# Two expert products whose matmuls keep their written order

## The chip, the cores and the metric

The kernel runs on one core of one Trainium2 chip. What is measured is the device time of one execution in microseconds (us). The kernel before was timed three times: 1403.73, 1405.36 and 1406.20 us, a median of 1405.36 us.

## The reference

One encoder block for 256 tokens of width 1024, all in float32: a conditioned RMS norm, a mixer (a gated delta rule with 8 heads beside a short convolution), a residual, a second norm, a mixture of experts, a residual and a last norm. Only the experts matter here. A router picks 4 of 32 experts for each token; each expert is two products with a clamped SwiGLU between them:

```
gu = x_blk @ w1[e] + b1[e]                  # 1024 -> 2048
gate, up = split(gu, 2)
gate = min(gate, 7); up = clip(up, -7, 7)
act = gate * sigmoid(1.702 * gate) * (up + 1)
y = act @ w2[e] + b2[e]                     # 1024 -> 1024
```

Every expert's 12 MiB of weights (8 MiB of w1, 4 MiB of w2) is read once, so the 32 experts need 384 MiB from HBM.

## The kernel before, in words

The program is written in a tile framework. It traces the whole kernel, and then a scheduler chooses the order of the instructions on each engine: it plays the program through a model of the engines and the transfers, and on each engine it takes next what its model says is ready, by priority. An instruction that went through `pin` (line 84, the scheduler's `keep_in_program_order`) keeps its written order with the other pinned instructions of its engine; unpinned ones may be put anywhere between them that their data allow. Semaphores are added by the framework.

The mixer runs up to about 430 us. After that come the experts, two at a time, in 16 pairs (p = 0 to 15; two pairs share a group q of gathered tokens). A pair's 128 token slots are four blocks of 32; `owners` says which of the pair's two experts owns each block (two and two, or three and one).

- First product (`w1_pair`, lines 1372 to 1388). For each of eight row blocks k of w1, two transfers of 1 MiB are issued, one for each expert (m = 0, 1). Then, for each of four column quarters c and each of four slot blocks j, a matmul multiplies 32 tokens (stationary operand, 128x32) with 512 columns of the owner's weights (moving operand, 128x512). Block j stands at column position 32*j of the array (`tile_position=(0, 32 * j)`), and its output in partitions 32*j to 32*j+31 of the bank `pss[c]`. A float32 matmul shows as two matmul records, so one k is 32 records and a whole first product 256.
- SwiGLU on VectorE and ScalarE, then `to_ff` (lines 1390 to 1398): eight transposes on TensorE and two copies to the tile `aT`.
- Second product (`w2_pair`, lines 1417 to 1435): four chunks c of two transfers of 1 MiB, and for each chunk two row blocks, two halves h of 512 columns and four blocks j: 128 records. Then the outputs are scaled, weighted by the gates in `combine` (line 1404, eight records) and added to x1.
- The last pair's second product is `w2_cols` (lines 1437 to 1458), in three parts of 512, 256 and 256 columns with transfers of 512 and 256 KiB. Its matmuls are pinned already.

The written order (lines 1600 to 1616) is first product of p, second product of p - 1, `to_ff` of p; at the end second product of 14, first product of 15, `to_ff` of 15, `w2_cols`. Between these stand, unpinned, the bias matmuls that open the banks (line 119), the gather of the next group's tokens (line 1315, into one buffer XT), and the transposes of the gates (line 1347). Weights go to 18 tiles of 1 MiB in turn (`w_half`, lines 954 to 963); their transfers are all issued from SyncE's queue (SP), and a transfer is issued when the matmuls that read its tile's last content are done. Part of pairs 0 and 1 is loaded while the mixer runs.

Already pinned on TensorE, besides `w2_cols`, are some matmuls of the mixer, the first bias and ranking matmuls and the single-block gathers of pair 0. All stand in the written order ahead of, or between, the matmuls that the change touches.

Of the kernel before, what the change touches and what calls it, by code (L numbers as in the profile page):

```python
# [21 lines left out]
KT = D // 128  # L22
# [31 lines left out]
def encoder_block(ctx, tc, x, c, ada_w, ada_b, norm1_w, w_in, conv_qkv_w, a_log, dt_bias, onorm_w,  # L54
# [3 lines left out]
    V, A, G, PE = nc.vector, nc.scalar, nc.gpsimd, nc.tensor  # L58
# [25 lines left out]
    pin = tc.keep_in_program_order  # L84
# [28 lines left out]
    def acc():  # L113
        return pm.tile([128, 512], FT, name="acc", tag=next(accs), bufs=3)

    def w1_bias(pa, bsel, b1c, pss, parts=(0, 1, 2, 3), first=False, pinned=False):
        for c in parts:
            b = 32 * c
            i = PE.matmul(pss[c], bsel[b:b + 32, pa * 128:(pa + 1) * 128], b1c[b:b + 32], start=first, stop=not first,
                          tile_position=(b, 0), skip_group_check=True)  # L120
            if pinned:
                tc.keep_in_program_order(i)
# [9 lines left out]
    with ExitStack() as mix:  # L132
# [218 lines left out]
        for j in range(4):  # L351
# [12 lines left out]
            w = ep.tile([128, KT, 256], FT, name="raw", tag="raw", bufs=6) \  # L364
# [13 lines left out]
            for kk in range(2):  # L378
                k = 2 * j + kk
# [574 lines left out]
        def w_half():  # L954
            i = half_n[0] % (NHALF + 7)
            half_n[0] += 1
            if i < NHALF - 2 or NHALF <= i < NHALF + 2:
                return wp_box[0].tile([128, 2, 2, 512], FT, name="wst", tag="wst").rearrange("p a b n -> p (a b n)")
            if i == NHALF - 2:
                pair_box.append(wp_box[0].tile([128, 2, 2, 2, 512], FT, name="wst", tag="pair", bufs=1))  # L960
            if i < NHALF:
                return pair_box[-1][:, i - NHALF + 2].rearrange("p a b n -> p (a b n)")
            return (h_tile if i - NHALF - 2 in (0, 1) else raw_tile)([128, 2048], FT, "wst")
# [10 lines left out]
        def w1_load(p, k, regs):  # L974
            w = pre.pop((p, k), []) if p < 2 else []
            for m in range(len(w), 2):
                w.append(quarters(w1_tile(p, k, m, regs)[0]))
            return w
# [302 lines left out]
    for k, m, ts in ((KT - 2, 0, [fw, spare("pg"), spare("pgT")]), (KT - 2, 1, [spare("aT", 1024), spare("aT", 1024)]),  # L1281
                     (KT - 1, 0, [spare("g"), spare("g"), spare("u"), spare("th")]),
                     (KT - 1, 1, [spare("ysb"), spare("ysb"), e4])):
        c, qs = 0, []
# [23 lines left out]
    def gather_part(P, xq, ks):  # L1308
        p = misc()
        for kk, k in enumerate(ks):  # L1310
            o = p[:, kk * QS:(kk + 1) * QS]
            n = 0
            for t in range(2):
                for hx in (h2h, h2l):
                    i = PE.matmul(o, hx[:, t, k * 128:(k + 1) * 128], P[:, t],
                                  start=n == 0, stop=n == 3, skip_group_check=True)
                    n += 1
                    if len(ks) == 1:
                        pin(i)
            if k % 2:  # L1320
                V.tensor_scalar(xq[:, k], o, afc[:, k:k + 1], mod[:, 24 + k:25 + k], op0=OP.mult, op1=OP.add)
            else:
                A.activation(xq[:, k], o, AF.Identity, scale=afc[:, k:k + 1], bias=mod[:, 24 + k:25 + k])  # L1323

    def xq_tile():
        return work.tile([128, KT, QS], FT, name="XT", tag="XT", bufs=1)
# [25 lines left out]
    def owners(q):  # L1352
        return [m for m, g in enumerate(GROUPS[min(q, 1)]) for _ in range(g)]

    def swiglu(n, g_ps, u_ps):
        g = work.tile([128, 512], FT, name="g", tag="g", bufs=2)
        u = work.tile([128, 512], FT, name="u", tag="u", bufs=1)
        th = work.tile([128, 512], FT, name="th", tag="th", bufs=1)
        V.tensor_scalar(g[:n], g_ps[:n], 7.0, None, op0=OP.min)  # L1359
        A.activation(th[:n], g[:n], AF.Tanh, scale=0.851)  # L1360
        V.tensor_scalar(u[:n], u_ps[:n], 7.0, -7.0, op0=OP.min, op1=OP.max)
        V.scalar_tensor_tensor(g[:n], u[:n], 1.0, g[:n], op0=OP.add, op1=OP.mult)
        V.scalar_tensor_tensor(g[:n], th[:n], 1.0, g[:n], op0=OP.add, op1=OP.mult)
        return g
# [7 lines left out]
    def w1_pair(p, xq, bsel, pss, regs, mid):  # L1372
        q, pa = divmod(p, 2)
        own = owners(q)[4 * pa:4 * pa + 4]
        if p:
            w1_bias(pa, bsel, b1c, pss, first=True)
        for k in range(KT):
            w = w1_load(p, k, regs)
            for c in range(4):
                for j in range(4):  # L1380
                    PE.matmul(pss[c][j * 32:(j + 1) * 32], xq[:, k, (4 * pa + j) * 32:(4 * pa + j + 1) * 32],  # L1381
                              w[own[j] % 2][c], start=False, stop=k == KT - 1,
                              tile_position=(0, 32 * j), skip_group_check=True)
            if p == 0 and k < KT - 2:
                gather_part(P0, xq, (k + 2,))
            if k == 3:
                mid()
        return [swiglu(128, pss[half], pss[2 + half]) for half in range(2)]
# [11 lines left out]
    def combine(gt, ysb, c0, n):  # L1400
        for t in range(2):
            p = misc()
            for pa in range(len(ysb)):
                PE.matmul(p[:, 0:n], gt[pa][:, t], ysb[pa], start=pa == 0, stop=pa == len(ysb) - 1)  # L1404
            xv = x1[:, t, c0:c0 + n]
            V.tensor_tensor(xv, xv, p[:, 0:n], op=OP.add)  # L1406

    def w2_rows(p, m, regs):
        return moe_w2[0, 2 * p + m:2 * p + m + 1] if p < 2 else moe_w2[0, ds(regs[2 * (p % 2) + m], 1)]

    def scaled(ps, c0, n):
        y = work.tile([128, 512], FT, name="ysb", tag="ysb", bufs=2)[:, 0:n]
        V.tensor_tensor(y, ps[:, 0:n], gtf_box[0][:, c0:c0 + n], op=OP.mult)  # L1413
        return y


    def w2_pair(p, aT, gt, regs):
        q, pa = divmod(p, 2)
        own = owners(q)[4 * pa:4 * pa + 4]
        ys = [acc() for _ in range(2)]  # L1420
        for c in range(4):
            w = []
            for m in range(2):
                t = w_half()
                nc.sync.dma_start(t, w2_rows(p, m, regs)[:, 256 * c:256 * c + 256].rearrange("e (p i) n -> p (e i n)", i=2))
                w.append(t.rearrange("p (i n) -> p i n", i=2))
            for i in range(2):
                f = 2 * c + i
                for h in range(2):
                    for j in range(4):  # L1430
                        PE.matmul(ys[h][j * 32:(j + 1) * 32], aT[:, f, j * 32:(j + 1) * 32],  # L1431
                                  w[own[j] % 2][:, i, 512 * h:512 * h + 512], start=f == 0, stop=f == KT - 1,
                                  tile_position=(0, 32 * j), skip_group_check=True)
        for h in range(2):
            combine([gt[:, pa]], [scaled(ys[h], 512 * h, 512)], 512 * h, 512)

# [97 lines left out]
    xq = xq_tile()  # L1534
# [37 lines left out]
    def first_product(p):  # L1572
        nonlocal xq, bsel
        q, pa = divmod(p, 2)
        nxt = []
        if pa == 0 and q:
            _, regs[q] = nc.values_load_multi_w_load_instructions(
                pidx_i[0:1, 4 * q:4 * q + 4], engines=[mybir.EngineType.SP], min_val=0, max_val=NE - 1)

        def mid():  # L1580
            if p == 2:
                final_row()
            if pa == 1:
                if q + 1 < NQ:
                    gts[q] = gates_of(q)
                if q + 1 < NQ:
                    nxt.append(slots_of(q + 1))

        gs[p] = w1_pair(p, xq, bsel, [acc() for _ in range(4)] if p else pss0, regs[q], mid)
        if p == 0:  # L1590
            route_rest()
        if nxt:
            xq = gather(nxt.pop())
            bsel = bias_rows(q + 1)

    def second_product(p):
        w2_pair(p, aTs.pop(p), gts[p // 2], regs[p // 2])
# [22 lines left out]
    with tc.If(n_over > 0):  # L1620
        ov = work.tile([128, KT, 128], FT, name="over", tag="aT", bufs=2).rearrange("p b n -> p (b n)")
        V.tensor_tensor(rks[:, 0], rks[:, 0], capr[:, None, :].to_broadcast([128, 2, NE]), op=OP.subtract)
        with tc.For_i(0, NE, 1) as cp:
# [6 lines left out]
            with tc.For_i(0, nb, 1) as b:  # L1630
# [23 lines left out]
                for half in range(2):  # L1654
                    pss = [acc() for _ in range(2)]
                    for gu in range(2):
                        bs = slice(32 * (2 * gu + half), 32 * (2 * gu + half) + 32)
                        PE.matmul(pss[gu][0:32], ohe[bs].to_broadcast([NE, 32]), b1c[bs],
                                  start=True, stop=False, tile_position=(bs.start, 0), skip_group_check=True)
                    for k in range(KT):  # L1660
# [5 lines left out]
                        for gu in range(2):  # L1666
                            PE.matmul(pss[gu][0:32], xo[:, k], wo[:, gu], start=False, stop=k == KT - 1,
                                      skip_group_check=True)
                    act_t(32, swiglu(32, *pss), aTo[:, half * 4:half * 4 + 4, :])
                for half in range(2):  # L1670
                    y = acc()
                    for f in range(KT):
# [5 lines left out]
                                  skip_group_check=True)  # L1678
# [48 lines left out]
```

## Time and profile before

| | |
|---|---|
| median of three runs | 1405.36 us |
| the profiled execution | 1404.75 us |
| its span, first to last instruction | 1402.8 us |
| mean granted TensorE clock | 0.985 |
| TensorE matmul (PE) busy | 1358.1 us, 97% |
| TensorE weight load (PEld) busy | 692.8 us, 49% |
| VectorE / ScalarE / GpSimd busy | 513.4 / 279.4 / 151.0 us |
| HBM read | 486.82 MB |

The span is what the trace covers; the execution was 1.95 us longer. Busy time of an engine is the union of its instructions, so matmuls that run side by side in the array count once: a busy TensorE isn't necessarily a full one. A weight load or matmul whose number of columns is 32 uses a quarter of the array's columns. Granted clock 1.00 is the level of 2.4 GHz, 0.50 that of 1.2 GHz. DMA share is the mean busy share of the core's 16 DMA engines.

### The profile page before, as it was taken

How to read it: one execution, taken by the hardware profiler on the slowest of the kernel's cores; microseconds unless marked ns; L12 is line 12 of the kernel's file. 1: busy time of each engine (PE TensorE's matmuls, PEld its weight loads, DVE VectorE, ACT ScalarE, POOL GpSimd, SP SyncE). 2: the span in 40 equal slices, each digit the busy share in tenths (PEclk: the TensorE clock that was granted, in tenths of full speed). 3: DMA queues.
4: the chain of work that ended last, by engine and by line, in shares of the span. 5: the costliest groups of instructions: out<-in, count | busy, mean ns of one | idle time of the engine just before them, and what ended most of it. 6: DMA issues, size and time to landing. Idle time of an engine off the chain costs nothing. (4 is left out here: it accounts for less than half of the span.)

```text
span 1402.8 us, 24525 instructions
## 1 busy us (share of the span) xinstructions
PE 1358.1 (97%) x10250; PEld 692.8 (49%) x10251; DVE 513.4 (37%) x1018; ACT 279.4 (20%) x545; POOL 151.0 (11%) x126
## 2 busy tenths in 40 slices
PE   6999998999999999999999999999999999999996
PEld 4988897999994333233233333333333333333322
DVE  3387879876763322221203112120311212031112
ACT  3555553543642110010000000000000000000001
POOL 4555684000100000000000000000000000000000
PEclk9999999999998999999999999999999999999997
DMA  9968876346797899999999999999999999999990
GB/s 336 302 226 290 282 242 218 98 147 237 282 376 282 360 408 394 403 421 420 421 421 420 421 421 421 420 421 421 420 415 420 421 400 421 421 416 413 421 337 32
DMA packets 134708, 492.68 MB, mean 351 GB/s; under 512 B 11070, under 2 KB 68799, under 8 KB 86977
## 3 DMA queue, kind: packets, MB, share of 16 engines
q1 hardware_dynamic: 130548, 486.08, 88.0%
q10 hardware_dynamic: 4045, 4.98, 1.1%
q8 instruction: 82, 1.34, 0.4%
q14 instruction: 33, 0.27, 0.1%
HBM read 486.82 MB, written 4.21 MB: 350 GB/s over the span
## 5 line engine op out<-in xcount | busy, mean ns | idle before, releaser
L1381 PE MATMUL acc<-wst,XT 128*32 128x512 f32 x4088 | 543.4, 597 | 0.0
L1381 PEld LDWEIGHTS acc<-wst,XT 128*32 128x32 f32 x4088 | 153.8, 110 | 350.4 <-issue 341.0
L1431 PE MATMUL acc<-wst,aT 128*32 128x512 f32 x1920 | 244.7, 599 | 0.0
L313 PE MATMUL mm<-hh,wl 128*128 128x256 f32 (+1 forms) x520 | 149.3, 288 | 4.9 <-DVE wl L263 3.6
L311 PE MATMUL mm<-hh,wh 128*128 128x256 f32 (+1 forms) x520 | 151.3, 291 | 1.2 <-DVE cacc L556 1.2
L312 PE MATMUL mm<-hl,wh 128*128 128x256 f32 (+1 forms) x520 | 149.4, 287 | 0.0
L1359 DVE TENSOR_SCALAR g<-acc 128x512 f32<-128x512 f32 x32 | 21.5, 687 | 326.2 <-PE acc L1381 323.0
L1431 PEld LDWEIGHTS acc<-wst,aT 128*32 128x32 f32 x1920 | 68.4, 110 | 142.2 <-issue 136.0
L262 ACT CAST wh<-raw 128x1024 fp32r<-128x1024 f32 (+1 forms) x89 | 91.8, 1038 | 93.8 <-PE mm L312 55.0
L88 POOL TENSOR_TENSOR rs<-ss,half_m 128x2 f32<-128x2 f32 x3 | 2.1, 702 | 975.3 <-DVE ss L1689 910.7
L311 PEld LDWEIGHTS mm<-hh,wh 128*128 128x128 f32 (+1 forms) x520 | 100.2, 193 | 12.5 <-issue 8.1
L313 PEld LDWEIGHTS mm<-hh,wl 128*128 128x128 f32 (+1 forms) x520 | 99.9, 192 | 7.1 <-DVE wl L263 3.8
L312 PEld LDWEIGHTS mm<-hl,wh 128*128 128x128 f32 (+1 forms) x520 | 100.2, 193 | 0.9 <-issue 0.8
L1397 ACT ACTIVATE aT<-misc 128x512 f32<-128x512 f32 x32 | 17.9, 595 | 409.6 <-PE misc L1396 409.5
L263 POOL TENSOR_TENSOR wl<-raw,wh 128x1024 fp32r<-128x1024 f32 x36 | 87.7, 2444 | 71.7 <-ACT wh L262 65.7
L1413 DVE TENSOR_TENSOR ysb<-acc,gtf 128x512 f32<-128x512 f32 (+1 forms) x33 | 22.3, 675 | 147.5 <-PE acc L1431 132.7
L1406 DVE TENSOR_TENSOR x<-x,misc 128x512 f32<-128x512 f32 (+1 forms) x66 | 44.3, 671 | 84.6 <-PE misc L1404 84.6
L263 DVE TENSOR_TENSOR wl<-raw,wh 128x1024 fp32r<-128x1024 f32 (+1 forms) x53 | 63.8, 1208 | 24.2 <-ACT wh L262 23.9
L1360 ACT ACTIVATE th<-g 128x512 f32<-128x512 f32 x32 | 20.1, 629 | 250.2 <-DVE g L1359 209.9
L1404 PE MATMUL misc<-ysb,pgT 128*128 128x512 f32 (+1 forms) x132 | 64.7, 608 | 2.0 <-DVE ysb L1413 1.9
L1323 ACT ACTIVATE XT<-misc,mod,afc 128x256 f32<-128x256 f32 x32 | 16.9, 563 | 172.4 <-PE acc L1381 120.8
L556 DVE SCALAR_TENSOR_TENSOR cacc<-mm,col,cacc 128x254 f32<-128x254 f32 (+1 forms) x96 | 46.0, 480 | 9.0 <-ACT cacc L553 6.9
(391 smaller groups left out, 1424.5 us busy)
## 6 DMA issues: line engine op xcount, KB each, us to landing
wst<-in_moe_w_dram SPq DMA_DIRECT2D x372, 1024.0 KB, 16.6
raw<-in_w_in_dram SPq DMA_DIRECT2D x36, 1024.0 KB, 7.6
raw<-in_ada_w_dram SPq DMA_DIRECT2D x24, 1024.0 KB, 8.5
wst<-in_moe_w_dram SPq DMA_DIRECT2D x24, 256.0 KB, 6.7
wst<-in_moe_w_dram SPq DMA_DIRECT2D x11, 512.0 KB, 15.4
raw<-in_w_out_sc_dram SPq DMA_DIRECT2D x4, 1024.0 KB
raw<-in_w_up_a_dram SPq DMA_DIRECT2D x4, 1024.0 KB, 5.3
raw<-in_w_o_dram SPq DMA_DIRECT2D x4, 1024.0 KB, 10.2
```

Of the source, the lines that this page charges most:

```text
L262: a = A.copy(wh, src)
L263: b = (V if job.lo == "v" else G).tensor_tensor(wl, src, wh.bitcast(FT), op=OP.subtract)
L311: PE.matmul(ps, wh[:, k, :], ah[:, k, :], start=k == 0, stop=False, skip_group_check=True)
L312: PE.matmul(ps, wh[:, k, :], al[:, k, :], start=False, stop=False, skip_group_check=True)
L313: PE.matmul(ps, wl[:, k, :], ah[:, k, :], start=False, stop=k == KT - 1, skip_group_check=True)
L556: V.scalar_tensor_tensor(a[:, o0:o1], p[:, s0:s1], cw(j), a[:, o0:o1], op0=OP.mult, op1=OP.add)
L1359: V.tensor_scalar(g[:n], g_ps[:n], 7.0, None, op0=OP.min)
L1381: PE.matmul(pss[c][j * 32:(j + 1) * 32], xq[:, k, (4 * pa + j) * 32:(4 * pa + j + 1) * 32], w[own[j] % 2][c], start=False, stop=k == KT - ...
L1404: PE.matmul(p[:, 0:n], gt[pa][:, t], ysb[pa], start=pa == 0, stop=pa == len(ysb) - 1)
L1406: V.tensor_tensor(xv, xv, p[:, 0:n], op=OP.add)
L1413: V.tensor_tensor(y, ps[:, 0:n], gtf_box[0][:, c0:c0 + n], op=OP.mult)
L1431: PE.matmul(ys[h][j * 32:(j + 1) * 32], aT[:, f, j * 32:(j + 1) * 32], w[own[j] % 2][:, i, 512 * h:512 * h + 512], start=f == 0, stop=f == ...
```

## The change

Both inner matmuls go through `pin`, so the scheduler has to keep them in the written order, among themselves and with the other pinned instructions of TensorE. No instruction, operand, tile or transfer is added or removed.

```
             for c in range(4):
                 for j in range(4):
-                    PE.matmul(pss[c][j * 32:(j + 1) * 32], xq[:, k, (4 * pa + j) * 32:(4 * pa + j + 1) * 32],
-                              w[own[j] % 2][c], start=False, stop=k == KT - 1,
-                              tile_position=(0, 32 * j), skip_group_check=True)
+                    pin(PE.matmul(pss[c][j * 32:(j + 1) * 32], xq[:, k, (4 * pa + j) * 32:(4 * pa + j + 1) * 32],
+                                  w[own[j] % 2][c], start=False, stop=k == KT - 1,
+                                  tile_position=(0, 32 * j), skip_group_check=True))
...
                 for h in range(2):
                     for j in range(4):
-                        PE.matmul(ys[h][j * 32:(j + 1) * 32], aT[:, f, j * 32:(j + 1) * 32],
-                                  w[own[j] % 2][:, i, 512 * h:512 * h + 512], start=f == 0, stop=f == KT - 1,
-                                  tile_position=(0, 32 * j), skip_group_check=True)
+                        pin(PE.matmul(ys[h][j * 32:(j + 1) * 32], aT[:, f, j * 32:(j + 1) * 32],
+                                      w[own[j] % 2][:, i, 512 * h:512 * h + 512], start=f == 0, stop=f == KT - 1,
+                                      tile_position=(0, 32 * j), skip_group_check=True))
```

## Rows read from the trace of the kernel before

**Rows 1.** The page's 40 slices of 35 us: TensorE busy tenths, GB/s moved.
```profile
PE   6999998999999999999999999999999999999996
...
GB/s 336 302 226 290 282 242 218 98 147 237 282 376 282 360 408 394 403 421 420 421 421 420 421 421 421 420 421 421 420 415 420 421 400 421 421 416 413 421 337 32
```
**Rows 2.** Stretches: us, each engine's busy us (count), PEclk, DMA share, GB/s.
```profile
600.00:1000.00 400.00, 397.30 (x2829) 132.68 (x2832) 83.88 (x184) 26.19 (x47) 0.00 (x0) 1.00 1.01 421
1000.00:1340.00 340.00, 338.54 (x2390) 112.10 (x2386) 65.28 (x123) 18.46 (x33) 0.00 (x0) 1.00 1.01 417
```
**Rows 3.** SyncE's queue, 600 to 1340 us: who waited for what, us, times, longest.
```profile
SPq L1425 <- PE acc L1381: 149.2, 56, 6.1
...
SPq L968 <- PE acc L1431: 116.6, 39, 10.9
```
**Rows 4.** TensorE's timeline, four places: start us, us, line, records.
```profile
441.34 3.64 PE L1381 MATMUL acc<-wst,XT 128*32 128x512 f32 x32
...
568.70 13.92 PE L1431 MATMUL acc<-wst,aT 128*32 128x512 f32 x128
...
605.80 13.94 PE L1381 MATMUL acc<-wst,XT 128*32 128x512 f32 x128
...
943.25 3.63 PE L1381 MATMUL acc<-wst,XT 128*32 128x512 f32 x16
```
**Rows 5.** Groups by line, 600 to 1340 us: records, busy us, mean ns, idle.
```profile
L1381 PE MATMUL acc<-wst,XT 128*32 128x512 f32 x3034 | 416.7, 595 | 0.0
L1431 PE MATMUL acc<-wst,aT 128*32 128x512 f32 x1664 | 214.4, 599 | 0.0
...
L1404 PE MATMUL misc<-ysb,pgT 128*128 128x512 f32 x104 | 51.8, 619 | 0.0
...
L119 PE MATMUL acc<-b1c,bsel 32*128 32x512 f32 x96 | 28.8, 639 | 0.7 <-DVE u L1361 0.7
L1315 PE MATMUL misc<-P,h2h 128*128 128x256 f32 x96 | 27.3, 315 | 3.3 <-ACT XT L1323 3.3
L1315 PE MATMUL misc<-P,h2l 128*128 128x256 f32 x96 | 24.1, 282 | 0.0
...
L1396 PE MATMUL misc<-ident,g 128*128 128x128 f32 x97 | 15.5, 298 | 0.1
```
**Rows 6.** Weight transfers: count, KB each, median us from issue to landing.
```profile
wst<-in_moe_w_dram SPq DMA_DIRECT2D x372, 1024.0 KB, 16.6
...
wst<-in_moe_w_dram SPq DMA_DIRECT2D x24, 256.0 KB, 6.7
```
**Rows 7.** SyncE's timeline, last pair: w1's 16 issues, then w2's 24.
```profile
1289.83 36.45 SPq L968 DMA_DIRECT2D wst<-in_moe_w_dram  x16
1328.30 32.05 SPq L1448 DMA_DIRECT2D wst<-in_moe_w_dram  x24
```
**Rows 8.** TensorE's timeline, last pair: first product, then the parts of w2_cols.
```profile
1330.95 3.63 PE L1381 MATMUL acc<-wst,XT 128*32 128x512 f32 x16
...
1336.42 28.18 PE L1381 MATMUL acc<-wst,XT 128*32 128x512 f32 x240
...
1369.62 9.34 PE L1455 MATMUL acc<-wst,aT 128*32 128x512 f32 x64
...
1381.70 3.66 PE L1455 MATMUL acc<-wst,aT 128*32 128x256 f32 x64
...
1386.96 3.66 PE L1455 MATMUL acc<-wst,aT 128*32 128x256 f32 x64
```
**Rows 9.** Stretches of 5 us at the end, columns as in Rows 2.
```profile
1360.00:1365.00 5.00, 4.59 (x36) 1.20 (x28) 1.97 (x4) 0.63 (x1) 0.00 (x0) 1.00 0.82 265
1365.00:1370.00 5.00, 2.18 (x12) 1.48 (x16) 3.28 (x5) 1.50 (x3) 0.00 (x0) 0.74 0.01 2
1370.00:1375.00 5.00, 5.00 (x32) 1.18 (x28) 0.00 (x0) 0.32 (x1) 0.00 (x0) 0.58 0.00 0
```
**Rows 10.** A stretch of 2 us within the pairs, columns as in Rows 2.
```profile
682.00:684.00 2.00, 2.00 (x16) 0.63 (x10) 0.10 (x1) 0.00 (x0) 0.00 (x0) 0.50 1.02 426
```

## The prediction

> **What bounds the kernel now.** I read the slices of the page first. From slice 18 on, where the experts run, two things look full at once: TensorE is busy 9 tenths or more in almost every slice, and the transfers move 420 or 421 GB/s in most of them [rows 1]. The stretches give the numbers: from 600 to 1340 us TensorE is busy 397.3 + 338.5 = 735.8 of 740 us, and the DMA engines show a share of 1.01 at 421 and 417 GB/s [rows 2]. Only one of them can set the pace, so the question is which one waits. SyncE does: its two largest waits alone, for TensorE to release weight tiles, hold 149.2 + 116.6 us of these 740 [rows 3]. So the tiles are full, enough transfers are queued that the engines never run dry, and TensorE works some way behind.
>
> How full is the busy TensorE? The timeline tells. Where it runs 128 records of either product in a row it takes 13.94 or 13.92 us, and 32 take 3.64 us [rows 4]. Some 0.17 us of each is the tail of the last one (mean 592 to 599 ns [rows 5], in a run of many one starts each 0.11 us), so a record costs about 13.77 / 127 = 0.1084 us when four stand side by side. Elsewhere 16 records take 3.63 us, as long as 32 do [rows 4]. That is one expert's half of a row block: with two owned blocks of four, two column positions of the array work and two stand empty. The scheduler took them apart because in its model one expert's half of the block had landed and the other hadn't. Counted over 600 to 1340 us: 3034 + 1664 = 4698 records take 416.7 + 214.4 = 631 us [rows 5], and at 0.1084 us they would take 509. About 120 us of TensorE's busy time is half-empty array.
>
> **The end.** What the lag costs shows only there. The last pair's 16 transfers of w1 are issued from 1289.83 us, the last at 1289.83 + 36.45 = 1326.3 [rows 7]; with 16.6 us to landing [rows 6] the first lands at about 1306.4 and the last at about 1342.9. TensorE starts on them at 1330.95, 24.5 us after the first landing, and finishes at 1336.42 + 28.18 = 1364.6 [rows 8], 21.7 us after the last. By then nearly all is moved: 265 GB/s from 1360 to 1365 us, then 2 and 0 [rows 9]. From 1365 us to the span's end at 1402.8 the work is a chain on TensorE and VectorE with its data present. So a lag that costs nothing in the middle, where the transfers set the pace, is paid at the end.
>
> **The change, part by part.** It adds and removes no instruction, semaphore or transfer. What moves is TensorE's order.
>
> 1. *Packing.* What does a pair need when packed? Two products are 256 + 128 = 384 records; 384 x 0.1084 = 41.6 us. Beside them stand combine, bias, gather and transposes: 51.8 + 28.8 + 27.3 + 24.1 + 15.5 = 147.5 us in 740 us [rows 5]. A pair's transfers are 24 x 1.049 MB = 25.2 MB, at 421 GB/s 59.8 us, so 740 us are 12.4 pairs, and the rest is 11.9 us a pair (rather too much, since overlaps count twice). Packed, TensorE needs 53.5 us a pair against 59.8 us of transfers.
>
> 2. *The lag.* With 6.3 us to spare in each pair, a lag of 24.5 us is worked off in four pairs of the 12; afterwards TensorE waits for data. These waits are new, and behind each stand the next matmuls and whatever was put after them. While TensorE keeps up with the transfers this is hidden by the transfers themselves. Without that cover it would cost its own length; the bounds are 0 and the spare 6.3 us a pair, and I take 0, since the trace shows 4.2 us of idle TensorE in 740 us although the same gathers, evictions and transposes stand in the queue [rows 2].
>
> 3. *A block must wait for both halves.* Before, a landed half could be begun alone. Now the last row block of the last w1 starts when its second half is there. That is 32 records, 3.6 us [rows 4], after 1342.9: the last first product ends at 1346.5, not 1364.6, that is 18.1 us sooner. This is the main term.
>
> 4. *From there to the end* the chain is as before: SwiGLU and transposes to 1369.62, the parts of w2_cols at 1369.62, 1381.70 and 1386.96 [rows 8], then the last evictions and the final norm. Shifted by 18.1 us the parts begin at 1351.5, 1363.6 and 1368.9. Is their data there? Transfers are through at about 1364, the last landing at the latest 1328.30 + 32.05 + 6.7 = 1367.1 [rows 6, 7]. The last part still finds it, with some 2 us over. So what is late next is the same TensorE chain, not the transfers, and the shift is kept whole.
>
> 5. *Transfers.* With tiles released sooner the queue never lacks one. From 1000 to 1340 us the rate is 417, not 421 [rows 2]: 340 x 4 / 421 = 3.2 us are regained. Between 500 and 600 us some more dips could close. They are small, the bounds are 0 and 5 us (the two slices of 35 us at 394 and 403 against 421 [rows 1] give 3.7, the one before them some of the rest), and I take 0, because this stretch runs packed already (the runs of 128 of rows 4 stand just there).
>
> 6. *Order on other queues.* SyncE's issues keep their order, since their tiles come free in the written order; ScalarE and VectorE get the same work. The scheduler replays its model with the pins and may put unpinned pieces elsewhere: between -2 and +4 us at the end, which I take as 0, the order of rows 8 being the written one already.
>
> The sum: 1402.8 - 18.1 - 3.2 = 1381.5 us of span; the execution lies 1.95 us above its span, 1383.4. The profiled execution, 1404.75, is 0.6 below the median of 1405.36, so I forecast 1384 us.
>
> One thing the trace says of waiting: at the end, with TensorE busy 2.18 of 5 us, the granted clock is 0.74 in that stretch and 0.58 in the next [rows 9], and once within the pairs it is 0.50, the level of 1.2 GHz, for a stretch of 2 us [rows 10]. The Trainium skill, "TensorE: Matmul & The Clock Gate", section "Loop structure matters more than you think", warns of just what point 2 makes: a loop that waits for a transfer ahead of its matmuls runs them on a cold engine. By that rule the change trades half-empty columns for a slow clock, and its result is the second rival; the trace bears it out for the idle time at the end, and no row shows what it does to an engine that waits within the pairs.
>
> **Rivals.**
>
> *A. The transfers hide it all.* For: 421 GB/s without a break [rows 1, 2], so the middle cannot get shorter. Against: 38 us at the end have no transfers under them [rows 9]. If TensorE's lag stayed, by waits of 6.3 us or more a pair in the new order, the time would be the old one, 1405 us. The same time follows if the new order isn't what fills the array, for which the run of 16 in 3.63 us speaks against.
>
> *B. The clock falls (slower).* Place: the waits of point 2, in each pair. A drop as in rows 10 loses half of the 2 us shown there and something on both sides of it, 1.7 us by my estimate. The spare 6.3 us a pair holds 3.7 drops; with up to 3.7 nothing is lost but the lag stays. With six, TensorE needs 53.5 + 10.2 = 63.7 us a pair, 3.9 more than the transfers, and 12 pairs give 47 us: 1452 us. Against it: a TensorE that falls behind no longer waits, and a busy one had 1.00 over both stretches [rows 2].
>
> *C. Half the lag stays.* Stalls at the gathers or transposes eat most of the spare, so that the lag falls from 24.5 to some 12 us: the gain is 9 + 3, and the time 1393 us. For it: the scheduler's model is not the chip, and waits of TensorE's queue are in written order now.
>
> *D. More is gained.* The dips around 550 us close (5 us), and the engine is warm when w2_cols begins, where 0.58 over 5 us [rows 9] cost 2.1 us: 1384 - 7 = 1377 us, or lower.
>
> **How the numbers follow.** The forecast with its own range, 1378 to 1390 us (point 6 and the other half of the clock's 2 us on both sides), has 0.68; D 0.08; C 0.10; A 0.08; B 0.06. For 8 in 10 I reach a little to both sides of it, to 1372 for D and to 1395 for C; A, B and the far ends of C and D are left out. A change under 0.2% (2.8 us) can't be told from none in this kernel. Faster: the forecast, C, D and no more, 0.86; the same: 0.07; slower: 0.07, B and a little of A.
>
> **What would show it.** Packing: the busy time of the two products from 600 to 1340 us falls by about 120 us, to some 510, and no run of 16 takes 3.6 us. Lag: TensorE's idle time ends at weight transfers, some 6 us a pair from about pair 6 on, and SyncE no longer waits for TensorE but for earlier transfers. End: the last first product ends within 4 us of the landing of its last w1 transfer, the stretch without transfers shrinks from 38 us to about 20, and the rate over 1000 to 1340 us is 421. The prediction is wrong if the matmuls are packed and the last transfer still lies 35 us ahead of the end (A), or if the granted clock falls well below 1.00 between 700 and 1300 us (B).

## The result, and the profile after

The changed kernel takes 1386.18 us (median of four runs, 1385.33 to 1389.08) against 1404.79 us (four runs, 1403.73 to 1406.20): a ratio of 0.9871 [0.9853, 0.9888], 18 to 19 us less. The forecast was 1384 us, the range 1372 to 1395. The profiled execution, the slowest of the four, took 1389.08 us, its span is 1387.2 us, 15.6 below the span before, and the mean granted clock is 0.980.

The page's slices of 35 us after the change, TensorE busy in tenths and GB/s, answer to [rows 1]:

```profile
PE   6999998899999999999999998999989899997986
GB/s 336 307 231 280 297 235 232 99 122 261 244 370 268 361 337 391 421 420 420 420 420 420 421 420 420 421 421 421 420 421 420 420 421 420 421 420 421 421 394 187
```

From the 17th slice to the 38th the transfers now run at 420 or 421 GB/s without one dip, and the transfer-free end shrank: the last slice moves 187 GB/s, not 32. The stretches (columns as in [rows 2]), with an earlier one added:

```profile
430.00:600.00 170.00, 168.40 (x1286) 58.95 (x1288) 47.27 (x130) 15.82 (x32) 0.10 (x1) 0.95 0.92 372
600.00:1000.00 400.00, 383.10 (x2969) 125.99 (x2958) 87.25 (x188) 27.52 (x48) 0.00 (x0) 1.00 1.01 421
1000.00:1340.00 340.00, 314.31 (x2411) 98.77 (x2413) 63.13 (x118) 18.92 (x33) 0.00 (x0) 0.98 1.01 421
```

TensorE, idle for 4.2 of 740 us before, is idle for 16.9 + 25.7 = 42.6. The two products by line, 600 to 1340 us (records, busy us, mean ns, idle ahead and what ended it), beside [rows 5]:

```profile
L1381 PE MATMUL acc<-wst,XT 128*32 128x512 f32 x3190 | 382.9, 594 | 23.2 <-DMA wst<-in_moe_w_dram 23.1
L1431 PE MATMUL acc<-wst,aT 128*32 128x512 f32 x1664 | 203.5, 606 | 6.0 <-DMA wst<-in_moe_w_dram 6.0
```

156 records more in 586.4 us instead of 631.1. Before, TensorE was never idle ahead of them; now it is, for 29.2 us, and 29.1 of these end at a weight transfer. Another 13.3 us of the 42.6 stand ahead of bias sums and gathers and end at VectorE and ScalarE (4.0 before, [rows 5]).

SyncE's waits in the same 740 us (who waited for what: us, times, longest) have changed sides. Before, its largest wait for an earlier transfer, which [rows 3] leave out, was

```profile
SPq L968 <- DMA wst<-in_moe_w_dram: 147.9, 88, 3.0
```

and after the change there is little else:

```profile
SPq L968 <- DMA wst<-in_moe_w_dram: 371.4, 192, 3.1
SPq L1425 <- DMA wst<-in_moe_w_dram: 189.4, 96, 3.0
SPq L1425 <- PE acc L1381: 13.2, 20, 5.4
...
SPq L968 <- PE acc L1431: 5.8, 18, 0.8
```

The two waits for TensorE of 149.2 and 116.6 us are down to 13.2 and 5.8: SyncE issues as soon as an earlier transfer is through. TensorE follows the transfers, and not the other way round.

The end, TensorE's timeline (start us, us; idle before and what ended it), against [rows 8]:

```profile
1333.40 3.64 PE L1381 MATMUL acc<-wst,XT 128*32 128x512 f32 x32 [0.30 <-DMA wst<-in_moe_w_dram]
...
1343.37 3.64 PE L1381 MATMUL acc<-wst,XT 128*32 128x512 f32 x32 [1.39 <-DMA wst<-in_moe_w_dram]
1348.29 3.63 PE L1381 MATMUL acc<-wst,XT 128*32 128x512 f32 x28 [1.28 <-DMA wst<-in_moe_w_dram]
...
1356.61 8.20 PE L1455 MATMUL acc<-wst,aT 128*32 128x512 f32 x64
...
1367.54 3.66 PE L1455 MATMUL acc<-wst,aT 128*32 128x256 f32 x64
...
1372.81 3.66 PE L1455 MATMUL acc<-wst,aT 128*32 128x256 f32 x64
```

Each row block of 32 records (the trace lacks four of the last) now starts when its transfer lands and is done 3.6 us later. The last first product ends at 1348.29 + 3.63 = 1351.9 us, before at 1364.6: 12.7 us. From there to the span's end it is 35.3 us, before 38.2: 2.9 us. 12.7 + 2.9 is the whole difference of the spans. In a second profiled run of the change (`after_again` below, span 1382.9 us) the same two parts are 16.9 and 3.0 us.

### The profile page after: what moved, and what is told of

The parts are those of the page before. It is cut to its first block, busy times and chain, and to the rows that moved or that the text cites. A ratio compares the mean times of both kernels' runs of the same rounds, so it can differ in the third digit from the quotient of the medians.

```text
span 1387.2 us, 24522 instructions
## 1 busy us (share of the span) xinstructions
PE 1300.7 (94%) x10250; PEld 668.2 (48%) x10251; DVE 513.5 (37%) x1018; ACT 281.0 (20%) x545; POOL 151.2 (11%) x126
## 5 line engine op out<-in xcount | busy, mean ns | idle before, releaser
L1381 PE MATMUL acc<-wst,XT 128*32 128x512 f32 x4088 | 491.9, 598 | 25.9 <-DMA wst<-in_moe_w_dram 25.8
L1381 PEld LDWEIGHTS acc<-wst,XT 128*32 128x32 f32 x4088 | 132.7, 110 | 342.7 <-issue 284.8
L1431 PE MATMUL acc<-wst,aT 128*32 128x512 f32 x1920 | 231.4, 604 | 6.0 <-DMA wst<-in_moe_w_dram 6.0
L312 PE MATMUL mm<-hl,wh 128*128 128x256 f32 (+1 forms) x520 | 149.2, 287 | 0.0
L1431 PEld LDWEIGHTS acc<-wst,aT 128*32 128x32 f32 x1920 | 64.1, 111 | 159.8 <-issue 144.3
L1315 PE MATMUL misc<-P,h2h 128*128 128x256 f32 x128 | 37.0, 319 | 10.2 <-DVE XT L1321 5.2
## 6 DMA issues: line engine op xcount, KB each, us to landing
wst<-in_moe_w_dram SPq DMA_DIRECT2D x372, 1024.0 KB, 19.8
```

The lines of the kernel that those rows point to most:

```text
L312: PE.matmul(ps, wh[:, k, :], al[:, k, :], start=False, stop=False, skip_group_check=True)
L1315: i = PE.matmul(o, hx[:, t, k * 128:(k + 1) * 128], P[:, t], start=n == 0, stop=n == 3, skip_group_check=True)
L1381: pin(PE.matmul(pss[c][j * 32:(j + 1) * 32], xq[:, k, (4 * pa + j) * 32:(4 * pa + j + 1) * 32], w[own[j] % 2][c], start=False, stop=k == K ...
L1431: pin(PE.matmul(ys[h][j * 32:(j + 1) * 32], aT[:, f, j * 32:(j + 1) * 32], w[own[j] % 2][:, i, 512 * h:512 * h + 512], start=f == 0, stop= ...
```

## The experiments

All times are compared with the kernel before on the same chip in the same series (medians 1402.84, 1402.28 and 1402.64 us). "Lag theory": TensorE's delay behind the transfers, carried to the end, is the price, and the change removes it by working it off over the pairs.

**Where along the pairs does the gain arise?** Only the first eight pairs pinned (the same in both products):

```
-                    pin(PE.matmul(...
+                    (pin if p < 8 else (lambda i: i))(PE.matmul(...
```

> Only pairs 0 to 7 are pinned; pairs 8 to 15 are in the scheduler's own order. Lag theory: the lag of some 24 us is worked off within the first eight pairs, and afterwards a TensorE that is about as fast as the transfers cannot build it up again: 1386 to 1393 us, and the last first product ends within some 8 us of the landing of its weights. Rival 'local' (the gain is what the packed order saves in the last pair or two): 1403 to 1405 us, as the end is the kernel before's.

Measured: 1391.90 us, 0.9914 [0.9883, 0.9945]. Its last pair of first products, on the timeline:

```profile
1328.12 28.17 PE L1381 MATMUL acc<-wst,XT 128*32 128x512 f32 x240
```

That ends at 1356.3, 8.9 us behind the landing of its last w1 transfer (1347.4, read from the trace), about the 8 that the lag theory named; before it was some 21.7. From 600 to 1340 us TensorE waits for a weight transfer just once, at 845.8 us, where the change begins to (841.6): the lag was gone by then, most of what was gained is still there eight pairs later, and some lag has come back.

Only the last pair's first product pinned (`pin if p == NP - 1`, the second product not at all):

> Only the first product of the last pair is pinned, all else is in the scheduler's order. Lag theory: the last product starts as late as before, and packing its 16 half-empty slots saves 2 to 4 us: 1401 to 1404 us. Rival 'local': 1386 to 1390 us.

Measured: 1398.82 us, 0.9976 [0.9966, 0.9986]. 3.5 us of the 18: within the 2 to 4 us that the lag theory gave (its range in us was counted from the first series, which lay some 2.5 us higher), and far from what a local effect would have given. No profile of it is read.

**Which product?** Only the first one pinned:

> Only the first product's matmuls are pinned. Lag theory (packed matmuls give TensorE spare time, the spare time works off its lag behind the transfers, and the lag was paid at the end): two thirds of the half-empty slots are in the first product, so a pair still needs less than the 59.8 us of its transfers and the lag goes to zero: 1385 to 1390 us, with TensorE idle before weight transfers within the pairs. Rival 'last product' (the gain comes from the order of the second product and of what follows it): 1400 to 1405 us.

Measured: 1384.43 us, 0.9867 [0.9842, 0.9893], the whole gain. Its end, and its last long stretch:

```profile
1344.93 3.63 PE L1381 MATMUL acc<-wst,XT 128*32 128x512 f32 x28 [1.32 <-DMA wst<-in_moe_w_dram]
```
```profile
1000.00:1340.00 340.00, 321.54 (x2420) 102.37 (x2414) 61.95 (x116) 18.34 (x33) 0.00 (x0) 1.00 1.01 420
```

TensorE is idle for 18.5 us there, enough to be without lag at the end. Only the second one pinned:

> Only the second product's matmuls are pinned. Lag theory: the first product keeps most of its half-empty slots, a pair needs nearly what its transfers take, and the lag goes only in part or not at all: 1395 to 1405 us. Rival 'last product': 1386 us.

Measured: 1395.83 us, 0.9951 [0.9934, 0.9968], some 7 us. Timeline of the end:

```profile
1334.01 24.67 PE L1381 MATMUL acc<-wst,XT 128*32 128x512 f32 x208
```

It ends at 1358.7, 14.6 us behind its last landing (1344.1, read from the trace): the lag is partly worked off.

**Is it the four side by side, or merely a fixed order?** Both products pinned, but in the first one all quarters of one expert's blocks are written ahead of the other's:

```
-            for c in range(4):
-                for j in range(4):
+            for m, c in [(m, c) for m in sorted(set(own)) for c in range(4)]:
+                for j in [j for j in range(4) if own[j] == m]:
```

> Everything is pinned as in the change, but in the first product the four slot blocks no longer stand side by side: for each row block first all quarters of one expert's blocks, then all of the other's. Lag theory: the order is as fixed as in the change, but each slot of the array holds two blocks of four (three and one in every second pair), so a first product takes 55.5 us instead of 27.7 and a pair 81 us, 21 more than its transfers: 16 pairs give some 300 to 350 us more, 1690 to 1740 us, transfers at about 310 GB/s and no idle TensorE. Rival 'fixed order' (it is the fixed order that helps, through earlier releases of the weight tiles, not what stands side by side): 1386 to 1395 us.

Measured: 1434.90 us, 1.0227 [1.0195, 1.0258]. Both expectations missed: the order matters, but costs 49 us over the change and not the 300 and more that strict half-empty running would. The timeline shows why the cost is smaller. First this kernel, in pair 0, where gathers cut the product into row blocks, and in a long run later; then the changed one in pair 0 (a second run of it):

```profile
444.44 5.38 PE L1381 MATMUL acc<-wst,XT 128*32 128x512 f32 x32
...
928.76 23.37 PE L1381 MATMUL acc<-wst,XT 128*32 128x512 f32 x197
```
```profile
443.90 3.64 PE L1381 MATMUL acc<-wst,XT 128*32 128x512 f32 x32
```

A row block of two halves takes 5.38 us, not two times 3.6. In a run of 197 records it is 23.37 / 197 = 0.119 us a record, near the 0.109 of a packed run [rows 4]. The starts of the 32 records say how (read from the trace): for the first 1.7 us two start at a time, for the next 1.7 us four, then two again. So TensorE starts matmuls of free column positions that stand behind others in its queue: the second half of one expert's matmuls runs beside the first half of the other's. By this reading, which no run tried by itself, the array stands half empty only where something full-width (combine, gather, transpose) or a wait cuts the queue next to a half block. The price is still there: the transfers ran at 329 GB/s from 430 to 600 us and at 418 and 409 in the two stretches behind, the last w1 landed 25 us later than in the change, and the last first product ended 22.6 us behind it, at 1396.3.

**Can the gain be taken back by using up the spare time?** Four matmuls whose product nobody reads are put behind each of the 15 second products, into the kernel with the change:

```
+        spin = misc()
+        for _ in range(4):
+            PE.matmul(spin, aT[:, KT - 1], h2h[:, 0, 0:512].bitcast(FT), start=True, stop=True, skip_group_check=True)
```

> The change with the same four matmuls a pair. Lag theory: TensorE was busy 314 of 340 us from 1000 to 1340 us, 55.3 us a pair, so 3.8 us more still fit under 59.8: the lag is worked off later, and the time is that of the change or little more, 1385 to 1393 us, transfers at 420 GB/s, less idle before transfers. Rival 'only the end': the same, 1386 us. Without room to spare (TensorE's waits are not free time): 1430 us or more.

Measured: 1403.01 us, 0.9996 [0.9982, 1.0011], the time of the kernel before. Its stretches, the added line from 600 to 1340 us, SyncE's largest wait there and the end:

```profile
600.00:1000.00 400.00, 392.99 (x2881) 126.64 (x2874) 83.28 (x176) 27.07 (x47) 0.00 (x0) 1.00 1.01 417
1000.00:1340.00 340.00, 335.54 (x2493) 108.78 (x2492) 65.68 (x129) 19.26 (x34) 0.00 (x0) 0.99 1.01 421
```
```profile
L1436 PE MATMUL misc<-h2h,aT 128*128 128x512 f32 x104 | 49.7, 611 | 0.0
```
```profile
SPq L1425 <- PE acc L1381: 196.1, 62, 8.3
```
```profile
1348.07 21.65 PE L1381 MATMUL acc<-wst,XT 128*32 128x512 f32 x194
```

Eight records a pair (a float32 matmul leaves two), 49.7 / 104 x 8 = 3.8 us. The transfers still run at 417 and 421 GB/s, so the middle hides them; yet the lag stays: the first product ends at 1369.7, 18.8 us behind its last landing (1350.9, read from the trace), against 3.8 in the change (1348.1), and SyncE waits for TensorE again. The forecast had been a hidden cost, at 1385 to 1393 us, because all of TensorE's idle time was taken as time to spare; only some 3.7 us a pair are (step 2 below), and 3.8 use them up. TensorE never waits for a weight transfer from 600 to 1340 us here; its 11.5 us of idle time end, as far as the trace names an end, at VectorE and ScalarE.

With eight instead of four:

> The change with eight such matmuls a pair, 7.6 us. Lag theory: 55.3 + 7.6 = 62.9 us a pair is over the transfers' 59.8, the lag can't be worked off and comes back at the end, and the pairs take 3.1 us more each: 1430 to 1450 us. Rival 'only the end': 1386 to 1392 us.

Measured: 1457.54 us, 1.0377 [1.0341, 1.0413], some 7 us beyond the range of the lag theory and far from its rival. The transfers no longer set the pace:

```profile
600.00:1000.00 400.00, 396.70 (x2789) 128.80 (x2788) 78.86 (x171) 24.44 (x42) 0.00 (x0) 1.00 0.98 402
1000.00:1340.00 340.00, 335.55 (x2370) 108.70 (x2374) 61.10 (x124) 19.51 (x34) 0.00 (x0) 1.00 0.97 396
```

The same four in the kernel before:

> The kernel before, with four float32 matmuls of 128x128 by 128x512 added to each of 15 second products; their result is read by nobody. Eight records of that size took 3.8 us in a row. Lag theory: before, TensorE needs about as long for a pair as the transfers (59.3 us of 59.8), so it has nothing to spare and becomes the bound: 3.3 us a pair, 1440 to 1455 us, transfers near 400 GB/s in the middle. Rival 'only the end' (the transfers alone set the pace until the last pair, whatever TensorE does, and the change only made the end shorter): 1403 to 1410 us.

Measured: 1490.09 us, 1.0621 [1.0595, 1.0648], beyond what either theory expected.

```profile
600.00:1000.00 400.00, 398.67 (x2633) 129.30 (x2632) 75.17 (x158) 22.67 (x40) 0.00 (x0) 1.00 0.95 386
1000.00:1340.00 340.00, 338.00 (x2190) 112.16 (x2190) 61.56 (x130) 19.12 (x35) 0.00 (x0) 1.00 0.93 376
```
```profile
L1381 PE MATMUL acc<-wst,XT 128*32 128x512 f32 x2840 | 415.7, 595 | 0.0
```

TensorE had nothing to spare before: the rates fall to 386 and 376 GB/s. 15 pairs x 3.8 are 57 of the 87 us. The packing got worse besides: a record of the first product takes 415.7 / 2840 = 0.146 us here, 0.137 before [rows 5], and 256 of them in 15 pairs make 35 us, about the rest. From 600 to 1340 us other work cuts the two products 103 times here and 85 times before (counted from the trace), although fewer pairs fit in; that the added matmuls did this by cutting the queue was not tried by itself.

**Why did the last w1 land late, and what was lost early?** The change again, in the second series:

> The change itself beside the two variants on one chip: 1385 to 1389 us.

1386.55 us, 0.9888 [0.9867, 0.9910]. Pinned from the third pair on (`pin if p > 1`), so that the start keeps the old order:

> Pinned from pair 2 on; pairs 0 and 1 are in the scheduler's order. In the change the transfers between 430 and 600 us move 372 GB/s against 385 before, 170 us x 13 / 421 = 5.2 us lost, beside a new order of the bias sums of line 1528 and the gather of the second group and a stretch at half clock. If the pins in the first two pairs cause it and the transfers are the bound from there on, this version regains it: 1380 to 1383 us, and 385 GB/s in that stretch. If that early loss is made up by the lag anyway (tiles are full either way), it makes no difference: 1385 to 1387 us.

1382.19 us, 0.9856 [0.9839, 0.9872]. The intervals overlap. Stretch 430 to 600 us of the repeat, then of this one:

```profile
430.00:600.00 170.00, 168.01 (x1306) 58.79 (x1309) 47.03 (x129) 16.07 (x33) 0.10 (x1) 0.97 0.94 382
```
```profile
430.00:600.00 170.00, 170.00 (x1297) 57.18 (x1295) 48.10 (x132) 16.43 (x33) 0.24 (x3) 0.97 0.95 381
```

Equal rates: the 372 GB/s of the first profile of the change belong to that execution, hardly to the order. (TensorE was at 1.2 GHz for 6.8 us of it, from 495 us on; whether that held the transfers up is not shown.) Next, the last pair's second product as two halves of 512 columns with 1 MiB transfers, so that no smaller transfers follow the last w1:

```
-    PARTS = ((0, 512), (512, 256), (768, 256))
+    PARTS = ((0, 512), (512, 512))
...
-    for i, (c0, n) in enumerate(PARTS):
-        w2_cols(NP - 1, c0, n, aTs[NP - 1], gts[NQ - 1], regs[NQ - 1])
-        if i < len(PARTS) - 1:
-            finish_part(xf, i)
+    w2_pair(NP - 1, aTs[NP - 1], gts[NQ - 1], regs[NQ - 1],
+            lambda h: finish_part(xf, h) if h < len(PARTS) - 1 else None)
```

> The change, with the last pair's second product loaded and computed as in the other pairs: transfers of 1 MiB over whole rows instead of 512 and 256 KiB, both halves at once, the final norm's parts at the end. In the change the transfers fall to 330 to 367 GB/s from 1340 us on, where these smaller pieces begin. If they also hold up the last transfers of w1, which land about 8 us later than predicted, the last w1 lands some 3 us sooner and the weights are through 5 us sooner; against it stand 3 to 5 us of norm and combine that no longer hide under the parts. Lag theory with the end bound by the chain behind the last w1: 1382 to 1388 us; if the overlap of the parts is worth more than the transfers: 1388 to 1393 us.

1385.10 us, 0.9885 [0.9868, 0.9902]. Its last row block, then that of the repeat:

```profile
1343.57 3.63 PE L1381 MATMUL acc<-wst,XT 128*32 128x512 f32 x28 [1.33 <-DMA wst<-in_moe_w_dram]
```
```profile
1344.05 3.63 PE L1381 MATMUL acc<-wst,XT 128*32 128x512 f32 x28 [1.32 <-DMA wst<-in_moe_w_dram]
```

Half a microsecond: the smaller transfers behind it do not hold up the last w1. Both edits together:

> Pins from pair 2 on and the last second product in whole rows, together. Each alone gave 1382.2 and 1385.1 us beside 1386.6 for the change and 1402.3 for the kernel before. If the two gains are real and independent: 1380 to 1382 us; if they were spread between runs: 1383 to 1387 us.

1381.06 us, 0.9844 [0.9824, 0.9863], the fastest measured and faster than both kernels. Its interval overlaps the change's first one (0.9853 to 0.9888) and lies just below the second; that it beats the change by some 4 us is likely, not settled.

The spans against the end of the last first product (both read from the trace of each profiled run with the same end of the program) sum it up:

| kernel | last first product ends | span ends | between |
|---|---|---|---|
| before | 1364.6 | 1402.8 | 38.2 |
| the change | 1351.9 | 1387.2 | 35.3 |
| the change, repeated | 1347.7 | 1382.9 | 35.2 |
| from the third pair on | 1349.2 | 1384.4 | 35.3 |
| first product only | 1348.6 | 1383.5 | 34.9 |
| second product only | 1358.7 | 1394.1 | 35.4 |
| first eight pairs | 1356.3 | 1391.9 | 35.6 |
| owner by owner | 1396.3 | 1433.7 | 37.4 |
| the change and four matmuls | 1369.7 | 1405.4 | 35.7 |
| the change and eight matmuls | 1420.1 | 1455.2 | 35.1 |
| before and four matmuls | 1451.0 | 1488.0 | 37.0 |

The time from there on is 34.9 to 38.2 us whatever came before, while the last first product is through between 1347.7 and 1451.0. What separates the kernels is when it is through. The 2 to 3 us more in three of the rows are looked at under step 4.

## Why the prediction was right, by its steps

The total and the mechanism held: 1386.2 against 1384. Its terms did less well, and their errors partly cancel: the last first product was to end 18.1 + 3.2 = 21.3 us sooner and ended 12.7 us sooner (16.9 in the repeat), and the end gave 2.9 us that the sum did not have. That the total came so close is in part luck.

One reading of the start was off: the two waits of [rows 3] are SyncE's two largest for TensorE, but its second largest of all was the 147.9 us for an earlier transfer. SyncE was held back at times, not always. The argument stands, since such a wait too means that transfers were queued.

**Step 1, packing: the term that was mis-sized.** The products' busy time was to fall to some 510 us; it fell to 586.4. At 0.1084 us a record the 4854 records would take 526, so 60 us over the packed time remain, of 122. The forecast that no run of 16 takes 3.6 us came true; what remains shows in the timeline of the changed kernel:

```profile
644.63 1.92 PE L1381 MATMUL acc<-wst,XT 128*32 128x512 f32 x16
646.48 1.98 PE L1404 MATMUL misc<-ysb,pgT 128*128 128x512 f32 x4
648.40 3.63 PE L1381 MATMUL acc<-wst,XT 128*32 128x512 f32 x30
651.96 1.13 PE L1404 MATMUL misc<-ysb,pgT 128*128 128x512 f32 x2
653.02 1.05 PE L1381 MATMUL acc<-wst,XT 128*32 128x512 f32 x4
654.00 1.12 PE L1404 MATMUL misc<-ysb,pgT 128*128 128x512 f32 x2
```

Blocks are full now, 16 records in 1.92 us, but combine and transposes are still dealt between them singly, and four records alone take 1.05 us, not 0.43. Other work cuts the two products 80 times from 600 to 1340 us, 85 times before (counted from the trace). The prediction packed everything perfectly, as if there were no cuts. A pair's products take 256 x 382.9 / 3190 + 128 x 203.5 / 1664 = 46.4 us, not 41.6. The rest of TensorE's busy time is 697.4 - 586.4 = 111 us, 9.0 a pair instead of the 11.9 counted with overlaps: 55.4, not 53.5.

**Step 2, the lag: right, at a lower rate.** 59.8 - 55.4 = 4.4 us are left in a pair, not 6.3, and not all of that is to spare: of the 25.7 us idle in the 5.7 pairs between 1000 and 1340 us, 20.8 end at weight transfers, 3.7 a pair, and 4.9 at VectorE and ScalarE (TensorE's waits, read from the trace). At 3.7 a pair 24.5 us take between six and seven pairs, not four; TensorE's first wait for a weight transfer is at 841.6 us, in the first product of pair 7, where the prediction had said about pair 6. The waits of the written order, taken at 0, cost no transfer rate, as 421 GB/s across them shows, but they use up spare time: those for VectorE and ScalarE grew from 4.0 to 13.3 us in 740. That the end pays for the lag is shown by the four added matmuls: they use up the spare time, leave the transfers at 417 and 421 GB/s from 600 us on, and cost 16.5 us. Of the 17.8 us by which their last first product ends later, 15.0 are lag and 2.8 a later landing.

**Step 3, the last first product: right in kind, late by landing.** It ends 3.8 us after its last landing, as foreseen, but at 1351.9. Foreseen were 1346.5, less the 3.2 of step 5: 1343.3. Of the 8.6 us, 5.6 are transfers: 480 MB were moved at 1335.8 us, before at 1333.4 (counted from the trace), not at 1330.2; the stretch from 430 to 600 us ran at 372 instead of 385 GB/s, which is 170 x 13 / 421 = 5.2 us. In the repeat 480 MB were there at 1331.6, and the first product ended at 1347.7. The other 3 us are the landing itself. The page's row for the 1 MiB transfers, beside [rows 6]:

```profile
wst<-in_moe_w_dram SPq DMA_DIRECT2D x372, 1024.0 KB, 19.8
```

19.8 us instead of 16.6: with SyncE hardly ever held back, eight are in flight nearly all the time. In 109 of the 111 cases from 600 to 1340 us in which the trace has that landing, a weight transfer is issued within 0.4 us of the landing of the eighth before it; in the kernel before in 41 of 111. And 8 x 1.049 MB at 421 GB/s are 19.9 us. The prediction had taken over the old landing time.

**Step 4, the chain at the end: better than foreseen, by luck as far as is known.** It was to keep its length, and shrank from 38.2 to 35.3 us. The parts start 10.9 and 5.3 us apart, before 12.1 and 5.3 [rows 8], and after the last start it is 14.4 instead of 15.8. For the first part the clock explains it: in about its first 5 us the granted clock was 0.58 [rows 9]; now it is 0.66, with transfers still under way, and 1.00 behind it (stretches of 5 us, columns as in [rows 9]):

```profile
1355.00:1360.00 5.00, 4.45 (x28) 1.65 (x32) 0.49 (x1) 0.60 (x1) 0.00 (x0) 0.66 0.95 317
1360.00:1365.00 5.00, 4.80 (x48) 1.11 (x40) 0.12 (x1) 0.00 (x0) 0.00 (x0) 1.00 0.97 319
1365.00:1370.00 5.00, 4.37 (x52) 2.19 (x56) 3.24 (x5) 1.45 (x4) 0.00 (x0) 1.00 0.81 265
1370.00:1375.00 5.00, 4.45 (x70) 2.47 (x65) 1.94 (x5) 1.02 (x4) 0.00 (x0) 1.00 0.00 2
```

The first part takes 8.20 us instead of 9.34 for it, which is what rival D had hoped for; but over the profiled runs it takes from 7.07 us (first product only) to 9.57 (owner by owner), so one profile of each kernel doesn't show that the change did it. The 1.4 us after the last start are the output: up to its first issue on ScalarE's queue it is 9.2 us in both, from there to the span's end 6.6 before and 5.2 after, and 5.2 to 6.4 in the other profiled runs. The stretch without transfers begins at about 1369 us and lasts 18, not 38. The last parts found their data, as forecast.

**Step 5, transfers:** 417 became 421 GB/s from 1000 to 1340 us, as forecast; the dips between 500 and 600 us did not close, and in the profiled run they grew by 5 us, an early loss below the bound of 0 that the step had set. **Step 6, other queues:** the scheduler did place the unpinned work elsewhere: from 600 to 1340 us combine stands in lone halves of two records six times, twice before, while the gathers went from 30 pieces to 11 (counted from the trace). What such pieces cost is in step 1.

**The rivals.** A (the transfers hide all) and C (half the lag stays) are out by the last row block that starts as its transfer lands. A's condition, a lag that stays, is what the four added matmuls made, and the time was A's. B, the clock, did not come as a loss of time: over the stretches with 42.6 us of waiting the granted clock is 1.00 and 0.98 at 421 GB/s, and the one larger drop between 1000 and 1340 us, 0.71 here, cost no transfer rate to speak of:

```profile
1150.00:1160.00 10.00, 9.12 (x42) 2.10 (x36) 4.73 (x7) 1.17 (x2) 0.00 (x0) 0.71 1.01 417
```

There are somewhat more drops than before: from 600 to 1340 us TensorE is at 1.2 GHz for 10.2 us in all (13.6 in the repeat), before for 3.4, the drop of [rows 10]. With only the first product pinned, where TensorE waits too, there is none, so that the waits bring them is not shown. Waits of some 1.3 us ahead of one row block after another thus left the clock at its upper level, apart from such single drops. The warning of the Trainium skill, "TensorE: Matmul & The Clock Gate", section "Loop structure matters more than you think", is of a long wait for a transfer ahead of every matmul, and no run here has that within the pairs, where the longest wait of TensorE in the change was 1.4 us.

## What to carry to other kernels

Where transfers set the pace and an engine is full too, look at how far that engine stands behind them: here the delay was free in the middle and was paid at the end, and some 3.7 us to spare in each pair removed it, while 3.8 us more work put it back. As time to spare, count only the idle time that ends at a transfer. A busy share of 99% does not say that TensorE is full: multiply its records by what one takes in a packed run and compare with the busy time. When a transfer queue is no longer held back, each transfer lands later, so use the landing time of a full queue in a forecast.

## What the runs showed of the hardware

TensorE starts matmuls of other column positions that stand behind waiting ones: 32 records in two half-width groups, one written behind the other, took 5.38 us, side by side 3.64, and a single half-width group of 16 took 3.63 [rows 4]. Four records alone between full-width instructions took 1.05 us, in a packed run 0.43. 1 MiB transfers landed in 19.8 us with eight in flight, and in 16.6 (medians) where SyncE was at times held back, at 421 and 417 to 421 GB/s.
